# A decoder step on one core: order of loads, operand splits and evictions around the MLP's block products, and the sample's matmuls in runs

## The chip, the core and the metric

The kernel runs on one core of a Trainium2 chip. Its engines take their instructions in program order, each from its own queue: PE (matmuls; its weight loads are PEld), DVE (vector), ACT (scalar), POOL (GpSimd) and SP, which here issues the DMAs. The metric is the device time of one execution in microseconds (us); lower is better.

## The reference

One step of a hybrid decoder trunk with one layer, for a prompt of 1024 tokens and 8 sample tokens which share the weights (`D_MODEL` 1024, `D_FF` 4096, all fp32). Cut to its frame:

```python
h = modulate(x, sh1, sc1)                       # adaLN on an RMS norm
q, k, v, z, xbc, dt_raw = split(h @ w_in)       # one combined projection
attn = merge of three dilated-window attentions over q, k, v
y, h_last = SSD over xbc, dt, starting from state_ssm   # 16 heads x 64 x 128 per sequence
mix = concatenate([rms_norm(attn) * g_attn, rms_norm(y * silu(z)) * g_ssm]) @ w_out
x = x + g1 * mix
u = jnp.square(jax.nn.relu(modulate(x, sh2, sc2) @ w_up))
x = x + g2 * (u @ w_down)
return rms_norm(x) * g_final, caches and states
```

## The kernel before

**Products.** An fp32 product is made of three matmuls of rounded parts (`mm3`): high by high (L63), high by low (L64), low by high (L65). A weight operand is therefore split on the way in: `split` lets ACT cast the high part (L52, tile `oh` for weights, `bo` or `th` for activations) and DVE subtract it from the source to leave the low part (L53, `ol`, `bo`, `tl`). L63 and L64 need the cast, L65 the subtraction too.

**MLP.** Its two matrix products run by a Strassen-Winograd scheme, with seven block products for each pair `q` of weight tiles (16 pairs). A product of the up projection is 4 k-steps of `mm3`, 12 matmuls into one PSUM bank of 128x512; six such banks rotate. The operands of the seven products are the blocks a11, a12, a21, a22 of two weight tiles `mr` and differences of them that POOL forms in place (L1825 to L1831). The generator `up_prep` does for each `q`: load the next pair, the sample tokens' matmuls on the raw tiles (`sample_up`, 16 matmuls with 32 rows), the differences, and one split at each `yield`. `step()` asks it for the next split; `need(key)` asks until that operand is there. For `q` below `EARLY` = 4 the first two products of each pair are done ahead (they need no transformed activations), so the rounds 0 to 3 have five products and the other twelve have seven.

**Order in a round.** `product` (L1978) issues the 12 matmuls, calling `hook(k)` behind each k-step, and then the eviction of the bank, `evict` (L1929): DVE adds the PSUM bank to a partial sum, and for four of the seven products `square` lets ACT do a ReLU and a square in place (L1923, L1924). In the loop over `q` and `j` the hook calls `step()` at k = 1, and at k = 0 and 2 `pop_later`, which issues what the evictions put off into the list `later`: POOL's differences of activations and SP's stores of them to DRAM (`u_d`). The products done ahead for `q` = 2 and 3 run beside `t_prep`, which forms the transformed activations ("hops" 2 to 6) and splits them, one tile at a hook.

**Seam.** In the last up round, `first_b(j)` starts the down projection: `b_pump` and `r_pump` issue loads of activation blocks (tiles `ub`) and of down weights (tiles `mr`) as slots allow, `b_split` splits an activation block. `down_prep` is the generator of the down projection's operands: for each chunk `c` of up to four pairs, product `j` and pair `k` it pumps both lists, calls `sample_down` for the sample's matmuls of a raw weight tile (4 matmuls, into one bank `sd`), splits the weight operand, forms POOL's differences, and splits the activation block.

**Down projection.** `phase_down` runs, for each chunk and product, four row blocks `m` of up to 48 matmuls; behind each it calls `step()`, evicts (adds into `U`, `V3`, `V5`, `P0`, or `gate`: the gated residual into `x1`, L2150), and pops up to five of `later`. In the last chunk the eviction of product 5 puts four POOL adds and four gates for each `m` into `later`. Then the last pair `q` = 15 is done without the scheme ("n" products, three PSUM banks `macc`), with the final norm between them.

**Two places ahead of the MLP.** `sample_ssd` works through the eight sample sequences' SSD states, one step at a time: each step loads a state (`stS`, 4 slots) and a broadcast row (`bbS`, 3 slots) two steps ahead on SP's queue, in between the loads of `qw_raw` for the q/k columns of the input projection and the stores of the caches. `h2_stats` forms, during the output projection, the row statistics of the second norm: after `wait` units of other work PE sums the squares (L1576), DVE and ACT take the root, and after another wait PE spreads it (L1581).

## Time and profile before

| | us |
|---|---|
| median of three runs | 2003.25 (2003.15 to 2004.2) |
| the profiled execution | 2005.3 |
| its span, first to last instruction | 2003.4 |
| PE busy | 1836.5 (92%) |
| DVE busy | 1221.8 (61%) |
| ACT busy | 802.2 (40%) |
| POOL busy | 711.3 (36%) |

The busy shares are means over the whole span; the stages have different limits. On the time axis of the profile the SSD states are worked on around 640 to 740 us, the output projection ends at about 1211, the first block products run until about 1280, the up projection until 1613, and the down projection until 1928, with the tail behind it. In the rows below an instruction is named by engine, line, operation, output tile <- input tiles, and shape; a bracket gives the engine's idle time just ahead of it and what ended that. A window's row gives the stretch and its length, then for PE, PEld, DVE, ACT and POOL the busy time with the number of instructions, then TensorE's granted clock as a share of its full speed, the mean busy share of the DMA engines, and what they moved. A grouped line gives the number of instructions, their busy time with the mean of one in ns, and the idle time ahead of them by releaser.

### The profile page before, as it was taken

How to read it: one execution, taken by the hardware profiler on the slowest of the kernel's cores; microseconds unless marked ns; L12 is line 12 of the kernel's file. 1: busy time of each engine (PE TensorE's matmuls, PEld its weight loads, DVE VectorE, ACT ScalarE, POOL GpSimd, SP SyncE). 2: the span in 40 equal slices, each digit the busy share in tenths (PEclk: the TensorE clock that was granted, in tenths of full speed). 3: DMA queues.
4: the chain of work that ended last, by engine and by line, in shares of the span. 5: the costliest groups of instructions: out<-in, count | busy, mean ns of one | idle time of the engine just before them, and what ended most of it. 6: DMA issues, size and time to landing. Idle time of an engine off the chain costs nothing.

```text
span 2003.4 us, 32735 instructions
## 1 busy us (share of the span) xinstructions
PE 1836.5 (92%) x12252; PEld 1526.1 (76%) x12252; DVE 1221.8 (61%) x2533; ACT 802.2 (40%) x1875; POOL 711.3 (36%) x590
## 2 busy tenths in 40 slices
PE   5999999999999798998889995899999989999976
PEld 3679999999999796766758984566667758778756
DVE  4613675675776667888634446544444465777896
ACT  3511334354422226877522334334443435334322
POOL 0010143342320644999200123454455440531440
PEclk7999999999999899999999997899999989999988
DMA  9674656466334777884573212688787799898712
GB/s 276 255 269 144 212 160 190 165 190 203 115 116 137 186 204 210 196 212 122 170 234 100 86 58 64 216 269 267 256 270 263 250 373 368 298 337 311 278 57 85
DMA packets 249771, 409.28 MB, mean 204 GB/s; under 512 B 35968, under 2 KB 183040, under 8 KB 243169
## 3 DMA queue, kind: packets, MB, share of 16 engines
q1 hardware_dynamic: 246028, 393.82, 60.4%
q0 software_dynamic: 3376, 13.30, 2.1%
q8 instruction: 96, 1.57, 0.3%
q14 instruction: 63, 0.52, 0.1%
q10 hardware_dynamic: 208, 0.07, 0.0%
HBM read 339.76 MB, written 201.65 MB: 270 GB/s over the span
## 4 chain that ended last, share of the span: by engine, by line
PE 67%; DVE 11%; DMA 7%; ACT 6%; POOL 4%; issue 4%; SPq 1%; POOLq 0%; DVEq 0%; ACTq 0%
PE acc L65 18%; PE acc L63 18%; PE acc L64 17%; DVE ol L53 3%; PE s L1294 2%; PE o L1332 2%; PE pt L1316 2%; DMA aw<-in_w_ada 1%; ACT oh L52 1%; DMA q_d<-ab 1%; ACT ub L1923 1%; PE y_ps L868 1%; PE y_ps L861 1%; DMA dkv<-in_cache_v_win 1%; DMA vw_raw<-in_w_in 1%
## 5 line engine op out<-in xcount | busy, mean ns | idle before, releaser
L53 DVE TENSOR_TENSOR ol<-mr,oh 128x512 fp32r<-128x512 f32 x186 | 164.0, 882 | 128.3 <-ACT oh L52 127.3
L64 PE MATMUL acc<-bo,oh 128*128 128x512 f32 (+1 forms) x484 | 186.6, 385 | 15.1 <-DVE bo L53 15.1
L63 PE MATMUL acc<-bo,oh 128*128 128x512 f32 (+1 forms) x484 | 189.6, 392 | 8.8 <-DVE x L2150 6.6
L63 PE MATMUL acc<-h_hi,cw_hi 128*128 128x352 f32 (+1 forms) x576 | 191.8, 333 | 1.1 <-ACT cw_hi L470 1.1
L65 PE MATMUL acc<-bo,ol 128*128 128x512 f32 (+1 forms) x484 | 185.6, 384 | 0.0
L64 PE MATMUL acc<-h_lo,cw_hi 128*128 128x352 f32 (+1 forms) x576 | 184.1, 320 | 0.0
L65 PE MATMUL acc<-h_hi,cw_lo 128*128 128x352 f32 (+1 forms) x576 | 183.7, 319 | 0.2 <-DVE cw_lo L471 0.2
L63 PE MATMUL acc<-h_hi,qw_hi 128*128 128x256 f32 (+1 forms) x512 | 151.7, 296 | 0.0
L65 PE MATMUL acc<-h_hi,qw_lo 128*128 128x256 f32 (+1 forms) x512 | 146.9, 287 | 2.0 <-DVE qw_lo L471 2.0
L64 PE MATMUL acc<-h_lo,qw_hi 128*128 128x256 f32 (+1 forms) x512 | 147.0, 287 | 0.0
L65 PE MATMUL acc<-th,ol 128*128 128x512 f32 x320 | 129.4, 404 | 14.8 <-DVE ol L53 14.7
L52 ACT CAST bo<-ub 128x512 fp32r<-128x512 f32 x109 | 67.5, 619 | 170.0 <-PE acc L65 150.4
L63 PE MATMUL acc<-th,oh 128*128 128x512 f32 x320 | 130.9, 409 | 4.1 <-ACT oh L52 4.1
L64 PE MATMUL acc<-tl,oh 128*128 128x512 f32 x320 | 125.6, 392 | 0.0
L63 PEld LDWEIGHTS acc<-bo,oh 128*128 128x128 f32 x484 | 93.7, 194 | 38.5 <-issue 14.0
L842 POOL TENSOR_TENSOR dec<-dec,CB 128x512 f32<-128x512 f32 x32 | 49.4, 1544 | 205.5 <-ACT dec L841 193.5
L1309 ACT ACTIVATE P<-P,st 128x256 f32<-128x256 f32 (+1 forms) x256 | 118.5, 468 | 2.9 <-DVE st L1298 2.8
L64 PEld LDWEIGHTS acc<-bo,oh 128*128 128x128 f32 x484 | 93.7, 194 | 33.9 <-DVE bo L53 18.0
L52 ACT CAST oh<-mr 128x512 fp32r<-128x512 f32 x186 | 112.9, 613 | 12.0 <-POOL mr L1826 5.9
L1923 ACT ACTIVATE ub<-ub 128x512 f32<-128x512 f32 x60 | 38.0, 633 | 192.0 <-DVE ub L1946 89.5
L53 DVE TENSOR_TENSOR bo<-ub,bo 128x512 fp32r<-128x512 f32 x109 | 105.7, 970 | 12.1 <-ACT bo L52 12.1
L63 PEld LDWEIGHTS acc<-h_hi,cw_hi 128*128 128x128 f32 x576 | 108.4, 188 | 2.1 <-ACT cw_hi L470 1.4
(493 smaller groups left out, 5038.8 us busy)
## 6 DMA issues: line engine op xcount, KB each, us to landing
out_k_win_sample<-in_cache_k_win SPq DMA_DIRECT2D x120, 512.0 KB
out_v_win_sample<-in_cache_v_win SPq DMA_DIRECT2D x120, 512.0 KB
ub<-u_d SPq DMA_DIRECT2D x109, 256.0 KB
u_d<-ub SPq DMA_DIRECT2D x105, 256.0 KB
mr<-in_w_up SPq DMA_DIRECT2D x34, 512.0 KB
aw<-in_w_ada SPq DMA_DIRECT2D x16, 1024.0 KB
mr<-in_w_down SPq DMA_DIRECT2D x32, 512.0 KB
cw_raw<-in_w_in SPq DMA_DIRECT2D x24, 512.0 KB
```

Of the source, the lines that this page charges most:

```text
L52: self.nc.scalar.copy(hi, src)
L53: (eng or self.nc.vector).tensor_tensor(lo, src, f32(hi), op=OP.subtract)
L63: mm(ps, lhi, rhi, start=first, stop=False)
L64: mm(ps, lhi, rlo, start=False, stop=False)
L65: mm(ps, llo, rhi, start=False, stop=last)
L842: nc.gpsimd.tensor_tensor(dec, dec, CB.unsqueeze(1).to_broadcast([128, 4, 128]), op=OP.mult)
L861: nc.tensor.matmul(y[64 * a:64 * a + 64, 128 * j:128 * j + 128], xdt[:, h], G[:, h], start=True, stop=(c == 0))
L1294: nc.tensor.matmul(s[:, a, u, :ws[u]], cols(q, i + u, i + u + 1)[h], cols(k, lo, hi)[h], start=True, stop=True)
L1309: nc.scalar.activation(P, P, AF.Exp, bias=st[:, i + u, a, 0:1], scale=-1.0, accum_out=st[:, i + u, a, 1:2])
L1316: nc.tensor.transpose(p[:, b, a], Ps[m][:, u, a, 128 * b:128 * b + 128], self.ident)
L1332: nc.tensor.matmul(o[64 * a:64 * a + 64, i % 4], v[:, lo + b, 64 * a:64 * a + 64], PT[:, b, a], start=(b == 0), stop=(b == hi - lo - 1))
L1923: nc.scalar.activation(t, t, AF.Relu)
```

## The change

The state and row loads of `sample_ssd` are issued three steps ahead instead of two, with one more slot each. The waits of `h2_stats` are longer. The first weight loads of `up_prep` are issued when the generator is made. In `phase_up`, a product's eviction is held and issued behind the first k-step of the next product; the split of the next operand moves from behind the second k-step to behind the first, ahead of that eviction, and `later` is popped at k = 1 and 3; for `q` = 3 of the products done ahead the split moves from behind the product into it. In the last up round the loads of the down projection start one product earlier, eight activation blocks are split where there were four, and `need((0, 0, 2))` stands ahead of the last eviction. `sample_down` is called once for several tiles: in chunk 0 for all eight, in the other chunks once for each half. At the end of the down projection POOL's adds are issued with the eviction, the gates are put off and popped one at a time, also during the "n" products, which have four PSUM banks. The diff, with context left out:

```diff
@@ -1014,15 +1014,15 @@
...
         def load(b):
-            st = sb.tile([128, 8, 128], F32, name="stS", tag="stS", bufs=4)
+            st = sb.tile([128, 8, 128], F32, name="stS", tag="stS", bufs=5)
             nc.sync.dma_start(st, I["state_ssm"][0, b].rearrange("(hp a) p n -> (a p) hp n", a=2))
-            bb = sb.tile([128, 8, 128], F32, name="bbS", tag="bbS", bufs=3)
+            bb = sb.tile([128, 8, 128], F32, name="bbS", tag="bbS", bufs=4)
             nc.sync.dma_start(bb, bass.AP(tensor=self.bc_d.tensor, offset=self.bc_d.offset + b * 128,
...

-        load(0)
-        load(1)
+        for b in range(3):
+            load(b)
         yield 3000
@@ -1036,8 +1036,8 @@
...
                 nc.gpsimd.tensor_tensor(t2, BB, g4(xd[:, :, b]), op=OP.mult)
-                if b + 2 < NB:
-                    load(b + 2)
+                if b + 3 < NB:
+                    load(b + 3)
                 yield 3200
@@ -1568,7 +1568,7 @@
...

-        def h2_stats(n, p, q, wait=5000):
+        def h2_stats(n, p, q, wait=8000):

@@ -1576,7 +1576,7 @@
...
             self.rstd(self.sm, rs[:, :nb], p[:, 0:nb], [128, 4], "r2")
-            yield 2500
+            yield 4000
             for i in range(nb):
@@ -1722,7 +1722,7 @@
...
         eo.close()
-        return lambda p: chain(h2_stats(2, p, p[:, 128:], 4000), h2_cols(2, p[:, 128:], 600))
+        return lambda p: chain(h2_stats(2, p, p[:, 128:], 4500), h2_cols(2, p[:, 128:], 600))

@@ -1769,7 +1769,7 @@
...
         prep = chain(self.up_prep(), self.down_prep())
-        done = set()
+        done = {next(prep)}

@@ -1809,6 +1809,7 @@
...
         load(0)
+        yield None
         for q in range(2, self.EARLY):
@@ -1975,9 +1976,16 @@
...

+        held = []
+
         def product(q, j, ps, w, hook):
-            self.mul(ps, w, hops[j], True, True, hook)
-            evict(q, j, ps)
+            def at(k):
+                hook(k)
+                if k == 0 and held:
+                    evict(*held.pop())
+
+            self.mul(ps, w, hops[j], True, True, at)
+            held.append((q, j, ps))

@@ -1996,9 +2004,13 @@
...
                 need((q, j))
-                product(q, j, bank(), self.ops.pop((q, j)), lambda k: next(side, None))
-                if q == self.EARLY - 1:
-                    step()
+
+                def hook(k):
+                    if k == 0 and q == self.EARLY - 1:
+                        step()
+                    next(side, None)
+
+                product(q, j, bank(), self.ops.pop((q, j)), hook)
         for q in range(16):
@@ -2006,12 +2018,11 @@
...
                 def hook(k):
-                    if k == 1:
+                    if k == 0:
                         step()
-                        next(side, None)
-                    if k in (0, 2):
+                    if k in (1, 3):
                         self.pop_later(1 + len(self.later) // 8)
-                    if q == 0:
+                    if q == 0 or k == 2:
                         next(side, None)
@@ -2019,6 +2030,8 @@
...
                     self.first_b(j)
+        need((0, 0, 2))
+        evict(*held.pop())
         self.pop_later(99)
@@ -2057,11 +2070,13 @@
...
             self.r_cap, self.b_live = 2, len(self.UB.parts) - 4
-        elif j == 2:
             self.b_pump()
...
         elif j > 2:
-            self.b_split((0, 0, j - 3))
+            for k in range(2):
+                self.b_split((0, (j - 3) // 2, 2 * (1 - j % 2) + k))
+                if j < 5:
+                    self.b_pump()
         if j == 5:
@@ -2074,16 +2089,15 @@
...
                 for k, q in enumerate(qs):
+                    if c or j > 1:
+                        self.b_pump()
                     if c + j:
-                        self.b_pump()
                         self.r_pump()
                     r1 = self.r_raw[c, 0, k]
-                    if j == 0:
-                        self.sample_down(2 * q, r1)
-                    else:
+                    if j:
                         r2 = self.r_raw[c, 1, k]
-                    if j == 1:
-                        self.sample_down(2 * q + 1, r2)
+                    if k == 0 and j < 2 and c + j:
+                        self.sample_down([(2 * p + h, self.r_raw[c, h, i]) for h in ((0, 1) if c == 0 else (j,)) for i, p in enumerate(qs)])
                     if j == 5:
@@ -2098,31 +2112,25 @@
...
                         self.r_live -= 1
-                    if c + j:
+                    if c or j > 1:
                         self.b_split((c, j, k))
...
             r = self.r_raw["n", i // 2]
-            if i % 2 == 0:
-                self.sample_down(30 + i // 2, r)
+            if i == 0:
+                self.sample_down([(30 + h, self.r_raw["n", h]) for h in range(2)])
             self.ops["n", i] = self.split_op(r[:, (lo, hi)[i % 2]])
...

-    def sample_down(self, slot, r):
-
-        if self.sdown is None:
-            self.held_s.append((slot, r))
-            return
-        for s, w in (*self.held_s, (slot, r)):
+    def sample_down(self, tiles):
+
+        for s, w in tiles:
             for j in range(4):
...
                                       start=(s == 0), stop=(s == 31))
-        self.held_s = []
-
-    held_s, sdown = [], None

@@ -2160,11 +2168,15 @@
...
             if j == 5 and c == len(self.CHUNKS) - 1:
-                add = lambda o, a, b: lambda: nc.gpsimd.tensor_tensor(o[:, m], a[:, m], b[:, m], op=OP.add)
-                self.later += [lambda: gate(m, h0, P0[:, m]), add(U, U, P0),
-                               lambda: nc.sync.dma_start(P0[:, m], self.x1_d[:, m + 4, h1]),
-                               add(V3, V3, U), add(U, U, V5), lambda: gate(m, h1, V3[:, m]), add(V3, V3, V5),
-                               lambda: gate(m + 4, h0, U[:, m]), lambda: gate(m + 4, h1, V3[:, m])]
+                for o, a, b in ((U, U, P0), (V5, U, V5), (U, U, V3), (V3, V3, V5)):
+                    nc.gpsimd.tensor_tensor(o[:, m], a[:, m], b[:, m], op=OP.add)
+                if m == 3:
+                    def c11(m):
+                        gate(m, h0, P0[:, m])
+                        nc.sync.dma_start(P0[:, m], self.x1_d[:, m + 4, h1])
+
+                    self.later += [lambda m=m: c11(m) for m in range(4)]
+                    self.later += [lambda m=m, t=t: gate(m + t[0], t[1], t[2][:, m]) for t in ((0, h1, U), (4, h1, V3), (4, h0, V5)) for m in range(4)]

@@ -2183,22 +2195,22 @@
...
                             evict(c, j, m, pss[m])
-                            self.pop_later(5)
+                            self.pop_later()
                             self.background()
...
                     del self.ops[c, j, k], self.b_ops[c, j, k]
-        self.pop_later(99)
         need(("n", 3))
         st = self.pool(el, "fin", bufs=2)
+        nc.scalar.copy(self.sa[:, 0:256], self.sdown[:, 0:256])
         ep.close()
+        esm.close()
         fps = self.pool(ep, "fps", bufs=4, space=PSUM)
-        acc = self.pool(ep, "macc", bufs=3, space=PSUM)
+        acc = self.pool(ep, "macc", bufs=4, space=PSUM)
         gb = st.tile([128, D], F32, name="gb", bufs=1)
...
         def sample_out():
-            nc.scalar.copy(ss[:, 0:256], self.sdown[:, 0:256])
             yield 1500
@@ -2220,6 +2232,7 @@
...
                 gate(m, slice(a, e), ps)
+                self.pop_later()
                 fin.advance(800)
@@ -2230,7 +2243,6 @@
...
         ep.close()
-        esm.close()

```

## Rows read from the trace of the kernel before

**Rows 1.** windows of three stages: us, busy by engine, PEclk, DMA, GB/s

```profile
1613.00:1654.00 41.00, 33.38 (x160) 21.84 (x160) 26.18 (x26) 15.44 (x29) 22.81 (x15) 0.83 1.01 374
1654.00:1928.00 274.00, 274.00 (x1313) 213.46 (x1313) 206.33 (x274) 108.38 (x203) 87.58 (x52) 1.00 0.81 296
1928.00:1960.00 32.00, 19.50 (x84) 15.28 (x83) 28.93 (x37) 1.22 (x3) 13.80 (x9) 0.73 0.10 33
```

**Rows 2.** windows of one early round and of ten later rounds, up projection

```profile
1281.13:1300.21 19.08, 16.34 (x92) 11.53 (x92) 9.78 (x12) 6.47 (x11) 11.36 (x9) 1.00 0.95 320
1357.24:1587.34 230.10, 218.12 (x1168) 161.17 (x1168) 106.92 (x145) 93.87 (x166) 110.61 (x81) 1.00 0.79 263
```

**Rows 3.** timeline of PE in a product: start, us, instruction, [idle <-releaser]

```profile
1422.25 0.39 PE L63 MATMUL acc<-th,oh 128*128 128x512 f32 x1
...
1424.29 0.39 PE L63 MATMUL acc<-th,oh 128*128 128x512 f32 x1
...
1425.37 0.39 PE L64 MATMUL acc<-tl,oh 128*128 128x512 f32 x1
1426.44 0.50 PE L65 MATMUL acc<-th,ol 128*128 128x512 f32 x1 [0.69 <-DVE ol L53]
```

**Rows 4.** timeline of PE around the sample's runs, down projection

```profile
1624.08 1.07 PE L2121 MATMUL sd<-mr,uS 128*32 128x256 f32 x16
1625.08 0.50 PE L63 MATMUL acc<-bo,oh 128*128 128x512 f32 x1
...
1703.82 0.39 PE L65 MATMUL acc<-bo,ol 128*128 128x512 f32 x1
1704.14 0.64 PE L2121 MATMUL sd<-mr,uS 128*32 128x256 f32 x8
...
1705.04 0.39 PE L64 MATMUL acc<-bo,oh 128*128 128x512 f32 x1
```

**Rows 5.** timeline of ACT around 1424, in the up projection

```profile
1423.84 0.63 ACT L1924 ACTIVATE ub<-ub 128x512 f32<-128x512 f32 x1
1424.38 0.60 ACT L52 CAST oh<-mr 128x512 fp32r<-128x512 f32 x1
```

**Rows 6.** lines of DVE, 1339 to 1613: busy us, mean ns, idle before them

```profile
L53 DVE TENSOR_TENSOR ol<-mr,oh 128x512 fp32r<-128x512 f32 x71 | 66.4, 935 | 80.7 <-ACT oh L52 79.9
...
L53 DVE TENSOR_TENSOR ol<-ms,oh 128x512 fp32r<-128x512 f32 x12 | 8.2, 682 | 0.0
```

**Rows 7.** timeline of PE at the first block products

```profile
1253.64 0.79 PE L63 MATMUL acc<-h_hi,oh 128*128 128x512 f32 x1 [21.61 <-ACT oh L52]
...
1262.34 0.50 PE L63 MATMUL acc<-th,oh 128*128 128x512 f32 x1 [2.10 <-ACT oh L52]
```

**Rows 8.** timelines of DVE and of ACT at the first block products

```profile
1241.93 6.66 DVE L53 TENSOR_TENSOR tl<-x,th 128x512 fp32r<-128x512 f32 x4
...
1252.97 0.62 ACT L52 CAST oh<-mr 128x512 fp32r<-128x512 f32 x1
```

**Rows 9.** timeline of PE around the row statistics

```profile
1197.62 0.81 PE L1576 MATMUL otr<-ones,sq 128*128 128x1 f32 x4 [3.11 <-POOL sq L1670]
...
1205.39 0.66 PE L1581 MATMUL otr<-ident,r 128*128 128x128 f32 x2 [2.94 <-DVE r L78]
```

**Rows 10.** timelines of SP and of POOL at the end of the up projection

```profile
1598.15 1.68 SPq L2039 DMA_DIRECT2D mr<-in_w_down  x2
...
1605.52 1.52 POOL L2094 TENSOR_TENSOR ms<-mr 128x512 f32<-128x512 f32 x1 [6.12 <-DMA mr<-in_w_down]
```

**Rows 11.** timeline of PE in the tail

```profile
1934.88 0.79 PE L64 MATMUL acc<-bo,oh 128*128 128x512 f32 x1 [5.45 <-DVE bo L53]
```

**Rows 12.** lines of DVE in the tail, 1914 to 1955

```profile
L2150 DVE SCALAR_TENSOR_TENSOR x<-U,mod,x 128x512 f32<-128x512 f32 x12 | 12.6, 1079 | 1.7 <-POOL U L2163 1.7
L53 DVE TENSOR_TENSOR ol<-mr,oh 128x512 fp32r<-128x512 f32 x8 | 8.7, 1088 | 0.0
```

**Rows 13.** waits of SP's queue, 640 to 740: us in total, times, longest us

```profile
SPq L1018 <- DMA out_ssm_sample<-stS: 14.6, 4, 6.0
```

## What the change is predicted to do, and how

> **What bounds the kernel now.** I read first the windows by stage, because the change touches only some of the 2003 us. Each line of that view gives a stretch's length, PE's busy time in it and the granted clock [rows 1]. From 1654 to 1928 us (the block products of the down projection) PE is busy all the time: only fewer PE slots help there. Over the seam between up and down projection (1613 to 1654) PE is busy 33.38 of 41.00 us at a clock of 0.83, and in the tail (1928 to 1960) 19.50 of 32.00, with DVE busy 28.93: DVE sets the time there. The second window view takes ten whole rounds of the up projection and one early round [rows 2]; PE looks nearly full in both, so "busy" doesn't show the loss and starts have to be counted. For that I read the timelines, PE's first (where does the start-to-start step grow, and who released it), then the timeline of the engine that is named there. Last come the grouped lines of DVE and the waits of SP.
>
> A time here is one of the profiled execution: 2005.3 us, its span 2003.4. The median of the runs is 2003.25, so gains are taken from 2003.25 as they stand. About 0.2% (4 us) is what a measurement of this kernel can tell from no change.
>
> **The change part by part.**
>
> *Up rounds (evict held until after the first quarter of the next product; the next split issued before it).* In a product PE starts a matmul every 0.227 us: nine starts from 1422.25 to 1424.29 take 2.04 [rows 3]. Ten rounds hold 70 products of 12, 840 matmuls, 190.4 us. The rest of their 1168 matmuls is the sample's [rows 2]: a run of 16 costs PE about 1.21 (1.00 from its start to the next product's, and 0.1 at either border [rows 4]), ten in all 12.1; some transposes are estimated at 1.1. Together 203.6, so of 230.10 there are 26.5 lost, 2.65 in each round. The loss sits in one pattern: ACT works in order, the cast `oh` of the next operand at 1424.38 stands behind the two activations of `square` that the evict issued [rows 5], DVE's subtraction `ol` waits for it, and PE's L65 waits for `ol` (0.69 at 1426.44, where the step from the matmul before it, at 1425.37, is 1.07 [rows 3]). In the whole stage DVE stood 79.9 us ahead of `ol` for that cast [rows 6], most of it hidden. After the change cast and subtraction are issued ahead of the evict, about 2.7 us before the product that needs them; the evict in its turn waits on ACT and DVE behind them, and behind the evict only the next one, with five more accumulators free. The pop of POOL's differences a quarter later delays stores, which have `later` to hide them. Only operand (q,2), which needs two POOL differences, stays marginal; I keep 0.2 of the 2.65. For 11.5 rounds (12 less the first's start and the last's end): 2.45 × 11.5 = 28. The three early rounds 1 to 3 have 60 matmuls and one sample run, 14.8, but one takes 19.08 [rows 2]. They are also held by the chain of POOL's differences (11.36 busy of 19.08), which stays; I take 17.6, a gain of 1.5 each, 4.5 in sum. **Up rounds: 32.5, from 24 (a third of the loss stays) to 37 (none).**
>
> *First block products (split issued inside the product).* PE idles 21.61 until 1253.64 and 2.10 until 1262.34, both on a cast `oh` [rows 7]. That cast (1252.97) is queued behind the operand casts of `t_prep` for hops 2, 3 and 4 and DVE's four subtractions (6.66 us from 1241.93) [rows 8]. Issued inside the product, it stands behind two of these hops: DVE is through at 1248.6, and with a subtraction of 0.68 [rows 6] PE starts about 1249.6, 4 earlier; the 2.10 goes, as its POOL difference is issued before and not behind the sample run. **6.5, from 3 to 10.**
>
> *h2_stats (longer waits).* PE waits 3.11 at 1197.62 for POOL's squares and 2.94 at 1205.39 for DVE [rows 9]. The longer wait puts the first behind 3 us more of products, so it goes; the second stays or is paid later. **3, from 0 to 6.**
>
> *First weight loads hoisted.* They are next in SP's queue as it is. **0.**
>
> *Sample's matmuls in runs.* A run of 8 between two products takes 1.22 from L65 at 1703.82 to the second matmul behind it at 1705.04; two matmul slots of 0.227 off that, 0.77. A run of 16 costs 1.21, so a merge of two saves 0.33 [rows 4]. Chunks 1 and 2 lose 6 borders each, chunk 3 loses 4: 16 × 0.33 = 5.3, where PE is busy throughout (274.00 of 274.00 [rows 1]). **5.3, from 4 to 6.**
>
> *Seam (first_b, down_prep).* The block splits of (0,1,k), 8 instructions, move into the last up round, and the pumps with them: each is a 256 KB load on SP's queue, ahead of stores of `u_d`. Of the 160 matmuls of the seam 96 are products and 64 are four runs of the sample's: 96 × 0.227 + 4 × 1.2 = 26.6 of bare work, so about 14 of its 41 us are lost [rows 1]. Against that: `need((0,0,2))` now stands ahead of the last evict, so that evict's ACT and DVE instructions queue behind the split of an operand whose weight tile may not have landed: a pair issued at 1598.15 released POOL at 1605.52, after 6.12 of idling, 7.4 us for the landing [rows 10]. Behind the evict wait the last stores and the pools' release; and the run of 8 tiles now waits for the last tile of the second half. **2, from −8 (that landing once in the open) to +5** (a third of the 14); I choose near the middle, since both mechanisms stand in the same 41 us.
>
> *Tail (adds at once on POOL, gates one at a time, a fourth bank).* DVE has 28.93 of 32.00 busy [rows 1] and does the same gates and splits after as before. What can go is its 1.7 of waiting for POOL's sums and about 0.8 of PE's 5.45 at 1934.88 [rows 11, 12]. The 16 adds in a row on POOL may slow DVE's splits, which take 1.088 in the mean there and 0.682 where POOL is quiet [rows 6, 12]. **2.5, from −2 (a dozen instructions slower by some 0.2) to +6 (the 5.45).** The Trainium skill ("SBUF — State Buffer", Who interferes with whom) says that a VectorE instruction with two inputs in SBUF and a GpSimd instruction that reads SBUF lock each other out for the whole instruction. The 0.682 against 1.088 agree; it speaks against this part and against the splits set beside POOL's differences, and is the mechanism of rival 1: without it the sum is the 51.8 below, by it rival 1's 36.
>
> *State loads three ahead.* In that stage SP waits 14.6 us in four waits, at most 6.0, until a state slot's store has drained [rows 13]; a fifth slot shortens these. The steps' number and POOL's work stay as they are. **0, from −6 (the longest of these waits moved onto the weight loads behind it) to +6 (the same wait gone from the path).**
>
> Sum: 32.5 + 6.5 + 3 + 5.3 + 2 + 2.5 + 0 = 51.8, so 2003.25 − 51.8 = 1951. With every low end 15 remain (1988), with every high end 76 (1927).
>
> **The rivals.**
>
> *1. Splits meet POOL (0.18).* `ol` now comes at the time of POOL's differences and is slower beside them (0.935 mean in this stage, 0.682 alone [rows 6]). If that eats half of the steady rounds' gain, 1.3 × 11.5 = 15 instead of 28, and the early rounds' 4.5 falls to 2: 2003.25 − 36 = 1967. For it: POOL is busy 110.61 of 230.10 [rows 2]. Against it: 2.7 us of slack for one slow subtraction.
>
> *2. The seam and the state loads cost (0.10).* The landing of 7.4 shows, and 6 is lost to the loads: 51.8 − 10 − 6 = 36, also about 1967.
>
> *3. More is freed (0.05).* The early rounds fall to 15 (+8), the seam and the first products give their high ends (+3, +4), h2 too (+3), and the tail gives 6 (+3.5): 51.8 + 21.5, about 1930.
>
> *4. Only the order of issue moves (0.03).* If the engines' waits, not their order, set the rounds (POOL's chain in each), all is hidden: 2003, within 0.2%. Against it: the cast's releaser is its own queue.
>
> *5. Slower (0.04).* A third pair of state loads stands in SP's in-order queue; where its slot is not free, the weight loads of the input projection behind it wait. There are eight steps; the gain of 52 is used up if each step is held by 6.5 us more than now, and 8 us more in each would give 2003.25 − 52 + 64 = 2015. Today's waits of 14.6 in all, 6.0 the longest [rows 13], with one slot more, speak against it.
>
> **How the numbers follow.** The terms hold (1938 to 1968): 0.60; rivals 1 and 2, 0.28, both at 1967 with a spread to 1980; rival 3, 0.05; rivals 4 and 5, 0.07. The forecast is 1951. Leaving out rivals 4 and 5, the slow half of the spread of 1 and 2, and part of 3, the range is 1930 to 1980. Faster by over 0.2%: 0.60 + 0.28 + 0.05 = 0.93; within it 0.03; slower 0.04.
>
> **What would show it.** In the profile of the changed kernel: ten steady rounds in about 206 us instead of 230.10, with ACT's `oh` ahead of the activations and no wait of L65 for `ol`; an early round near 17.6; the first block product's wait near 17.5 instead of 21.61; no wait for POOL's squares; 16 fewer runs of the sample's matmuls between 1654 and 1928, each remaining one of 16 taking 1.0 or longer; the seam not longer, with POOL's wait on the weight tile ahead of the last evict; the tail's DVE as busy as before, with no wait for POOL. Wrong it would be if the rounds stay above 215 (rival 1, if `ol` is then longer; rival 4, if not), if the seam grows past 41 (rival 2), or if the stretch from 640 us on gets longer (rival 5).

## The result, and the profile after

The changed kernel takes 1949.36 us in the median of four runs (1946.67 to 1951.71) against 2003.72 for the kernel before (2003.15 to 2004.54): a ratio of 0.9728, 95% interval 0.9711 to 0.9745. Its profiled execution took 1947.37 us, its span 1945.2. So the two traces differ by 58.2 us and the medians by 54.4; the rest is the choice of the executions.

PE issues its product matmuls in the same order in both kernels, so each of them can be found in both timelines. The table takes the start of the first matmul of each stretch and compares the lengths.

| stretch, with PE's start before / after | before | after | difference | term of the sum |
|---|---|---|---|---|
| to the SSD states' stage (625.15 / 623.45) | 625.15 | 623.45 | −1.7 | none |
| states, attention, first part of the output projection (to 1176.51 / 1177.30) | 551.36 | 553.85 | +2.5 | 0 |
| row statistics, to the first product of `q` = 2 (1223.10 / 1222.15) | 46.59 | 44.85 | −1.7 | −3 |
| first block products, to round 1 (1281.13 / 1274.76) | 58.03 | 52.61 | −5.4 | −6.5 |
| early rounds 1 to 3 (to 1337.53 / 1330.75) | 56.40 | 55.99 | −0.4 | −4.5 |
| rounds 4 to 15, to the last up product (1609.81 / 1572.51) | 272.28 | 241.76 | −30.5 | −28 |
| seam, to the end of the third down product (1665.17 / 1622.51) | 55.36 | 50.00 | −5.4 | −2 |
| down products, to the last of chunk 3 (1928.37 / 1880.26) | 263.20 | 257.75 | −5.5 | −5.3 |
| tail, to the end of the span (2003.4 / 1945.2) | 75.03 | 64.94 | −10.1 | −2.5 |

The sum is −58.2. The first line holds nothing that the change touches. The windows of the changed kernel for one early round, ten later rounds, the seam, and the tail ahead of and behind the first product of the last pair (columns as in the rows ahead of the prediction):

```profile
1274.76:1293.07 18.31, 16.38 (x92) 11.54 (x93) 8.92 (x12) 6.47 (x11) 11.06 (x9) 1.00 0.75 238
1351.12:1556.07 204.95, 204.95 (x1173) 166.11 (x1172) 116.60 (x144) 95.86 (x167) 118.13 (x80) 1.00 0.88 295
1572.51:1622.51 50.00, 41.45 (x221) 32.04 (x220) 30.74 (x35) 22.58 (x41) 23.76 (x15) 0.93 0.98 363
1880.26:1895.75 15.49, 8.34 (x38) 6.57 (x36) 15.49 (x17) 0.74 (x2) 10.61 (x7) 0.88 0.21 70
1895.75:1945.20 49.45, 36.32 (x266) 33.54 (x266) 39.30 (x96) 12.98 (x41) 0.00 (x0) 0.88 0.24 86
```

Before, the same two stretches of the tail were:

```profile
1928.37:1950.61 22.24, 12.00 (x45) 8.06 (x44) 21.72 (x24) 0.85 (x2) 13.43 (x9) 0.77 0.15 48
1950.61:2003.40 52.79, 35.61 (x266) 33.37 (x266) 35.74 (x89) 12.89 (x41) 0.00 (x0) 0.87 0.22 81
```

Ten rounds take 204.95 us against 230.10 [rows 2], and PE is busy in all of it. The early round, 18.31 against 19.08, has gained next to nothing. In the tail DVE is busy without a gap until the last pair's first product (15.49 of 15.49; before 21.72 of 22.24), and that stretch is 6.75 us shorter. Behind it DVE has more to do (39.30 against 35.74) in less time (49.45 against 52.79).

ACT's timeline in a steady round after the change, and DVE's group of weight subtractions from 1330 to 1573 us (lines view, as in [rows 6]):

```profile
1386.06 0.63 ACT L1924 ACTIVATE ub<-ub 128x512 f32<-128x512 f32 x1 [3.05 <-DVE ub L1947]
1386.72 0.63 ACT L1925 ACTIVATE ub<-ub 128x512 f32<-128x512 f32 x1
1387.26 0.60 ACT L52 CAST oh<-mr 128x512 fp32r<-128x512 f32 x1
```

```profile
L53 DVE TENSOR_TENSOR ol<-mr,oh 128x512 fp32r<-128x512 f32 x71 | 78.5, 1109 | 78.8 <-ACT oh L52 77.5
```

The cast still runs directly behind a pair of activations [rows 5], but behind the pair of one product earlier: it is through at 1387.86, when PE has the last matmuls of its product and a run of the sample's (at 1388.65) still ahead of it. The subtraction has become slower, 1.109 us in the mean against 0.935, and DVE's idle time ahead of it, 77.5 against 79.9, has hardly changed [rows 6]. Neither matters any more: PE waits for none of it.

### The profile page after: what moved, and what is told of

Same layout as the page of the kernel before. It is cut to its first block, busy times and chain, and to the rows that moved or that the text cites. A ratio compares the mean times of both kernels' runs of the same rounds, so it can differ in the third digit from the quotient of the medians.

```text
span 1945.2 us, 32764 instructions
## 1 busy us (share of the span) xinstructions
PE 1808.9 (93%) x12252; PEld 1535.4 (79%) x12252; DVE 1230.5 (63%) x2533; ACT 804.7 (41%) x1875; POOL 719.7 (37%) x590
## 4 chain that ended last, share of the span: by engine, by line
PE 67%; DVE 11%; DMA 7%; POOL 6%; ACT 4%; issue 3%; SPq 2%; DVEq 0%; ACTq 0%; POOLq 0%
PE acc L63 19%; PE acc L65 18%; PE acc L64 18%; POOL dkv L1111 2%; POOL dkv L1115 1%; PE s L1294 1%; PE pt L1316 1%; PE o L1332 1%; DVE tl L53 1%; DMA q_d<-ab 1%; DVE ol L53 1%; PE y_ps L868 1%; DVE x L2158 1%; PE y_ps L861 1%; DMA vw_raw<-in_w_in 1%
## 5 line engine op out<-in xcount | busy, mean ns | idle before, releaser
L53 DVE TENSOR_TENSOR ol<-mr,oh 128x512 fp32r<-128x512 f32 x186 | 180.6, 972 | 133.8 <-ACT oh L52 127.8
L63 PE MATMUL acc<-bo,oh 128*128 128x512 f32 (+1 forms) x484 | 185.6, 383 | 14.4 <-DVE x L2158 8.1
L64 PE MATMUL acc<-bo,oh 128*128 128x512 f32 (+1 forms) x484 | 183.5, 379 | 3.0 <-DVE bo L53 3.0
L64 PEld LDWEIGHTS acc<-h_lo,cw_hi 128*128 128x128 f32 x576 | 108.4, 188 | 0.6
L65 PEld LDWEIGHTS acc<-h_hi,cw_lo 128*128 128x128 f32 x576 | 108.2, 188 | 0.5 <-DVE cw_lo L471 0.5
```

Source lines behind the costliest of these rows:

```text
L53: (eng or self.nc.vector).tensor_tensor(lo, src, f32(hi), op=OP.subtract)
L63: mm(ps, lhi, rhi, start=first, stop=False)
L64: mm(ps, lhi, rlo, start=False, stop=False)
L65: mm(ps, llo, rhi, start=False, stop=last)
```

## The experiments

Each is an edit of the changed kernel, unless the text says otherwise. Medians within 3 us of each other are not told apart here, since the runs of one kernel spread by up to 8 us; what a single edit does is read from the stretches of the traces.

### The changed kernel once more

> The changed kernel once more, as the base for the variants beside it and to see where its own runs, which spread from 1946.67 to 1951.71 us, differ. If the spread comes from one place (theory: the order in which DMAs land in the SSD states' stage, 640 to 745 us, or at the start), this execution's PE starts differ from those of the first trace by up to 5 us there and by under 0.3 us in every up round, the seam and the tail. If the block products themselves vary, the rounds differ too.

Measured: 1949.2 us (1944.35 to 1951.49), ratio 0.9717 (0.9703 to 0.9732). The steady rounds, down products and the tail agree with the first trace to 0.05 us each. What differs is the states' stage with what follows (554.72 against 553.85 us), round 3 (18.14 against 19.33) and the seam (51.70 against 50.00). So the theory held for the steady rounds and the tail, and not for round 3 and the seam. Differences in the former are worth reading to a tenth, those in the seam only above 2 us.

### The split behind the held eviction again

```diff
                 def hook(k):
-                    if k == 0:
+                    if k == 1:
                         step()
```

> The changed kernel, but in the rounds 0 to 15 of the up projection the split of the next operand is issued behind the second k-step, so behind the held eviction and its two activations again; the eviction stays held. Theory 1 (the order of cast and activations on ACT's queue makes the steady rounds' gain): the rounds return from about 20.4 to about 22.9 us, some 28 us slower in 11 rounds, about 1977. Rival (holding the eviction, or popping POOL's differences a quarter later, makes the gain): the rounds stay near 20.4 and the time near 1949.

Measured: 1987.17 us, ratio 0.9909 (0.9896 to 0.9923). Ten rounds:

```profile
1360.95:1590.10 229.15, 218.19 (x1170) 161.18 (x1168) 111.55 (x144) 93.85 (x166) 110.59 (x81) 1.00 0.78 264
```

That is 229.15 us, where the kernel before had 230.10 [rows 2] and the changed kernel has 204.95. Holding the eviction and popping POOL's differences later gives 1 us of the 25; the place of the split, ahead of the activations on ACT's queue or behind them, gives the rest. The forecast was 28 us for the whole. The medians differ by 38, the traces of this kernel and the changed one beside it by 35.4: 29.2 in the rounds 4 to 15, 1.7 in the rounds 1 to 3, 4.2 in round 0 and the product ahead of it. Round 0 was not in the expectation.

### The split two products ahead, evictions not held

```diff
                     if k == 0:
-                        step()
+                        step(2 if (q, j) == (0, 2) else 1)
...
                 product(q, j, bank(), self.ops.pop((q, j)), hook)
+                if (q, j) != (15, 6):
+                    evict(*held.pop())
```

> The changed kernel, but evictions are not held in the rounds 0 to 15 (issued right behind their product, as in the kernel before) and the split is asked for two products ahead instead of one. Theory 1 in its general form (what counts is that cast and subtraction are through before the product that needs them): steady rounds at 20.4 or less, as the split still stands behind an eviction but has a whole product (2.7 us) more; the early rounds 1 to 3, 18.3 us each now, may fall towards 16, since POOL's chain starts a product earlier; the time 1941 to 1950. Rival (the eviction must stand behind the split, since the activations wait on PE's last matmul and hold the queue): steady rounds near 22.9, about 1977.

Measured: 1943.71 us, ratio 0.9694 (0.968 to 0.9707). An early round and ten later rounds:

```profile
1273.97:1288.94 14.97, 14.97 (x94) 12.01 (x92) 8.64 (x11) 6.74 (x12) 11.93 (x9) 1.00 0.90 299
1341.18:1546.51 205.33, 205.33 (x1173) 166.24 (x1172) 105.10 (x145) 95.30 (x168) 110.79 (x80) 1.00 0.89 291
```

The steady rounds take 205.33, as with the held eviction, so the rival falls: what counts is only that the split is through before its product, whichever way it is brought forward. The early round shown falls to 14.97, which is the bare work of 14.8; over the rounds 1 to 3 it is 46.8 us against 56.0 and 54.7 in the two traces of the changed kernel. What holds these rounds after the change shows in DVE's, ACT's and POOL's timelines of the changed kernel:

```profile
1274.74 1.23 DVE L53 TENSOR_TENSOR ol<-mr,oh 128x512 fp32r<-128x512 f32 x1 [6.04 <-ACT oh L52]
1275.89 0.68 DVE L1958 TENSOR_TENSOR ub<-acc,t 128x512 f32<-128x512 f32 x1
```

```profile
1274.09 0.62 ACT L52 CAST oh<-mr 128x512 fp32r<-128x512 f32 x1 [4.06 <-POOL mr L1827]
1276.60 0.63 ACT L1924 ACTIVATE ub<-ub 128x512 f32<-128x512 f32 x1 [1.89 <-DVE ub L1958]
1277.26 0.63 ACT L1925 ACTIVATE ub<-ub 128x512 f32<-128x512 f32 x1
1277.80 0.60 ACT L52 CAST oh<-mr 128x512 fp32r<-128x512 f32 x1
```

```profile
1270.16 1.29 POOL L1952 TENSOR_TENSOR ub<-ub,b 128x512 f32<-128x512 f32 x1 [12.37 <-ACT ub L1925]
...
1272.76 1.29 POOL L1827 TENSOR_TENSOR mr<-mr,ms 128x512 f32<-128x512 f32 x1
```

The split of operand (q,2) waits for a POOL difference (L1827). That one stands in POOL's queue behind an operation on activations out of `later` (L1952), which has waited 12.37 us for ACT's activations (5.31 and 5.32 in rounds 1 and 2). Only in round 3, where the split is round 4's, is it the sample's matmuls that POOL waits for (5.67). The split now stands ahead of an eviction whose bank is long done, so DVE idles 6.04 us with that eviction (L1958) behind it, and the next cast, at 1277.80, comes behind the late activations. This idling ahead of a ready eviction is new with the order. Asked for two products ahead, POOL's differences are issued ahead of L1952 (the first at 1267.56, that one at 1273.67) and no longer wait for the activations.

The gain of 10 us up to the last up product was partly lost at the seam (54.72 us against 50.00 and 51.70).

### One part of the change alone, on the kernel before

The eviction held, the split at the first k-step, the pops a k-step later; nothing else.

> The kernel before with one part of the change alone: in the up projection the eviction held, the split issued ahead of it behind the first k-step, the pops a k-step later. Nothing else. Theory 1: the steady rounds fall from 22.9 to 20.4 and the first block products as little as they may (the split stays behind the product there), so 28 us less in the rounds 4 to 15 and the time 1974 to 1978; seam and tail as in the kernel before, or the seam up to 3 longer as the last eviction comes later. Rival (other parts of the change share in the rounds' gain): rounds over 21.

Measured: 1977.36 us, ratio 0.986 (0.9847 to 0.9874).

```profile
1358.06:1563.04 204.98, 204.98 (x1173) 166.09 (x1172) 116.79 (x144) 95.73 (x167) 117.63 (x80) 1.00 0.88 295
```

Ten rounds take 204.98; from round 4 to the last up product it is 30.5 us less than before, exactly as in the whole change (−30.5). Seam, down products and the tail ahead of the last pair are as before within 1 us. The part stands alone and adds up with the rest.

### No request ahead of the last eviction

```diff
-        need((0, 0, 2))
         evict(*held.pop())
```

> The changed kernel without the request for operand (0,0,2) ahead of the last eviction of the up projection. Theory (the last eviction stands on DVE behind two splits whose weight tiles land late; PE's first down product waits 6.15 us for that eviction, the 8 us low end of the seam term): that wait falls to 1 to 2 us, and 3 to 5 us of it remain as a gain at the third block product, so 1944 to 1947 against 1949. Rival (the seam is bound by the loads behind it, so the request costs nothing net): the first wait falls but later waits of the same stage take it back, within 1 us at the third block product; or the next splits come later and it is slower by up to 3.

Measured: 1948.55 us, ratio 0.9722 (0.9707 to 0.9736), not to be told from the changed kernel. PE's and DVE's timelines of the changed kernel at that place, and PE's without the request:

```profile
1581.64 0.76 PE L63 MATMUL acc<-bo,oh 128*128 128x512 f32 x1 [6.15 <-DVE ub L1971]
```

```profile
1579.61 1.28 DVE L53 TENSOR_TENSOR ol<-mr,oh 128x512 fp32r<-128x512 f32 x2
1580.81 0.68 DVE L1971 TENSOR_TENSOR ub<-acc,u 128x512 f32<-128x512 f32 x1
```

```profile
1581.72 0.76 PE L63 MATMUL acc<-bo,oh 128*128 128x512 f32 x1 [4.93 <-DVE ub L1971]
```

The wait falls from 6.15 (7.88 in the second trace) to 4.93 and not to 1 or 2, because the eviction stands behind block splits of `first_b` too (on DVE they are from 1579.68 to 1580.97 in this run, the eviction starts at 1580.89). The seam takes 48.82 us against 50.00 and 51.70: 1 to 3 us, at the edge of what the seam's own spread allows.

### The old order of the activation blocks

The loads and splits in `first_b` and `down_prep` as before: four blocks split in the last up round, not eight.

> The changed kernel with the loads and splits of activation blocks in the last up round as before (four blocks split there, those of the second product's operands in the down projection). Theory (these four splits on ACT and DVE, issued while PE had no slack, are what the second block product of the down projection waited for, 20.55 us against 10.87 in the traces with the change): that product returns to 17 to 21 us, 6 to 10 slower, and the first gets up to 2 shorter. Rival (merging the sample's matmuls, or the earlier landing of loads, is what shortened it): it stays under 13.

Measured: 1955.0 us, ratio 0.9763 (0.9744 to 0.9782). The second down product in the kernel before, in the changed one and here:

```profile
1633.74:1654.29 20.55, 15.12 (x53) 11.07 (x50) 18.34 (x17) 8.19 (x16) 12.03 (x8) 0.75 1.03 393
```

```profile
1597.90:1608.78 10.88, 10.88 (x50) 9.01 (x48) 10.05 (x9) 6.09 (x11) 10.80 (x8) 1.00 1.09 401
```

```profile
1600.01:1618.52 18.51, 13.69 (x50) 10.36 (x48) 18.51 (x15) 6.62 (x13) 17.10 (x11) 0.82 1.04 396
```

It goes from 10.88 back to 18.51, with DVE busy in all of it, and the seam to 57.6 us. DVE was the bound of that product. Four subtractions less stand there now; beside POOL, which is busy 17.10 of the 18.51 us here, one takes about 1.75, so four make 7.0 of the 7.6 us. PE's granted clock is also higher with them gone (1.00 against 0.82 and 0.75).

### The tail's gates as before

The adds and gates put off together, popped five at a time and all ahead of the last pair; four banks and the early copy stay.

> The changed kernel with the tail's gates and adds put off and popped as in the kernel before (five at a time, all of them ahead of the last pair's products); four banks and the early copy of the sample's sum stay. Theory (twelve of the gates now run behind the start of the last pair's products, where DVE has room; ahead of it DVE sets the time, so what counts is the place of the gates and not their number): the stretch from the last chunk's product 6 to the first product of the last pair, 15.5 us now and 22.2 before, returns to 21 to 22, and the rest of the tail stays near 40.7 (44.1 before) or gains up to 2, so 5 to 7 slower than the changed kernel. Rival (the fourth bank carries the tail's gain): that stretch stays under 17 and the time within 2 us.

Measured: 1956.7 us, ratio 0.9766 (0.975 to 0.9782). The two stretches of the tail:

```profile
1882.66:1906.32 23.66, 12.08 (x38) 8.58 (x36) 23.13 (x27) 0.74 (x2) 12.98 (x8) 0.74 0.14 45
1906.32:1954.30 47.98, 35.51 (x266) 33.04 (x266) 33.64 (x86) 12.99 (x41) 0.00 (x0) 0.89 0.24 89
```

The first is 8.2 us longer than in the changed kernel, the second 1.5 shorter. So the place of the gates, with that of POOL's adds, which this edit moves too, makes 7 of the tail's 10 us. The rest (52.79 to 47.98 behind the last pair's first product, less what the first stretch is longer than the 22.24 of before) comes from the fourth bank, the early copy or both; these were not taken apart. In the groups of DVE ahead of the last pair, first before (from 1928.37 us), then after (from 1880.26):

```profile
L2150 DVE SCALAR_TENSOR_TENSOR x<-U,mod,x 128x512 f32<-128x512 f32 x8 | 8.7, 1122 | 0.5 <-POOL U L2163 0.5
...
L2150 DVE SCALAR_TENSOR_TENSOR x<-x,mod 128x512 f32<-128x512 f32 x2 | 3.5, 1758 | 0.0
```

```profile
L2158 DVE SCALAR_TENSOR_TENSOR x<-U,mod,x 128x512 f32<-128x512 f32 x3 | 2.6, 857 | 0.0
L2158 DVE SCALAR_TENSOR_TENSOR x<-x,mod 128x512 f32<-128x512 f32 x2 | 2.2, 1121 | 0.0
```

The ten put-off gates in this stretch, 12.2 us, have become five, 4.8 us. Nine of the sixteen now run behind the last pair's first product (one begins just ahead of it), where POOL does nothing, and take 0.741 in the mean. The expectation's "twelve" is not what the trace has.

### Two ahead, no request, and no gate ahead of the last pair

```diff
                             evict(c, j, m, pss[m])
-                            self.pop_later()
```

and the edits of the runs "The split two products ahead, evictions not held" and "No request ahead of the last eviction".

> Three edits on the changed kernel: evictions not held and the split two products ahead (as in the run of that alone), no request for operand (0,0,2) ahead of the last eviction, and none of the put-off gates issued ahead of the last pair's products (all of them popped between these). Theory: the first gives 9 to 10 us up to the last up product and loses up to 5 of them at the seam, where the last eviction again stands behind late weight tiles; the second gives those back; the third takes four gates of about 1.1 us out of the DVE-bound stretch, 15.5 to some 11 to 12 us. Sum 9 + 2 + 4 = 15 less than 1949, 1934. Rival (the tail's first gates then wait for the reload of the block that they use as scratch; the seam is bound by loads): 1941 to 1944, no better than the first edit alone.

Measured: 1941.12 us, ratio 0.9688 (0.9674 to 0.9703). The tail:

```profile
1872.95:1882.15 9.20, 8.33 (x38) 6.60 (x36) 9.20 (x10) 0.74 (x2) 8.89 (x6) 1.00 0.00 0
1882.15:1938.50 56.35, 36.19 (x266) 32.47 (x266) 45.07 (x102) 12.98 (x41) 1.91 (x2) 0.92 0.28 95
```

The first stretch falls to 9.20, and the second grows by 6.9: sum 65.55 against 64.94 in the changed kernel. The run with the split two ahead alone, which keeps the changed kernel's tail, has 65.57 (15.48 and 50.09), so moving the last gates out gives nothing. The rival was right in its result, by another way: PE now waits for DVE at the final norm's transposes behind the last pair's products. With all gates ahead of the last pair (71.64) DVE is the bound there; with some ahead or none the tail is equally long.

### Two ahead, every eviction first

As two ahead, with the last eviction too right behind its product and no request ahead of it.

> The changed kernel with the split two products ahead and every eviction of the rounds 0 to 15, the last one too, issued right behind its product; no request for operand (0,0,2) ahead of the last one; the tail as in the changed kernel. Theory (in the two runs with the split two ahead the last eviction stood behind block splits that waited for their loads, and PE's first down product waited 8.09 us for it): the first down product starts 2 to 5 us earlier than there, counted from the last up product (11.1 us), the 10 us up to there stay, so 1935 to 1938 against 1949. Rival (the splits of the first two down operands come as late anyway): the start moves by under 1 us, 1940 to 1942.

Measured: 1942.02 us, ratio 0.9686 (0.9673 to 0.9699). The wait of PE's first down product, in the run above and here, and the seam here:

```profile
1573.48 0.77 PE L63 MATMUL acc<-bo,oh 128*128 128x512 f32 x1 [8.09 <-DVE ub L1971]
```

```profile
1571.65 0.76 PE L63 MATMUL acc<-bo,oh 128*128 128x512 f32 x1 [5.27 <-DVE ub L1971]
```

```profile
1563.41:1616.30 52.89, 44.30 (x222) 33.46 (x220) 32.45 (x37) 22.36 (x41) 23.55 (x15) 0.90 1.03 391
```

Counted from the last up product the first down product starts after 8.2 us instead of 11.1, as the theory had it, and the seam still takes 52.89 against 52.79: later products give the 2.8 back, and the time is the rival's. The DMA engines are busy throughout (1.03), as they were before (1.01 [rows 1]). That the loads bound the seam once the up projection ends earlier is argued from this and was not tried by itself.

### Four differences on DVE instead of POOL

```diff
-            g(t2[k], b21[k], t2[k], op=OP.subtract)
+            v(t2[k], b21[k], t2[k], op=OP.subtract)
```

on the kernel of the run above.

> The kernel with the split two products ahead and every eviction first, and besides four differences of t_prep (128x512, L1898) on DVE instead of POOL. Theory (rival 1's mechanism, a subtraction with two inputs in SBUF and a POOL instruction take turns; in the changed kernel's round 0 five subtractions beside these four take 1.75 us instead of 0.68): the subtractions there take 0.68, the four differences cost DVE 2.7 us, and round 0 gets 1.5 to 3 us shorter. Rival (DVE is the bound of round 0 and the four more instructions cost what the others gain; or PE waits there for POOL's other differences): round 0 within 1 us or up to 2.7 longer.

Measured: 1940.68 us (1933.21 to 1941.36), ratio 0.9661 (0.9642 to 0.9679). DVE's timeline in the changed kernel, while POOL runs the four differences from 1251.00 to 1257.79, and then in this one:

```profile
1251.51 1.75 DVE L53 TENSOR_TENSOR ol<-mr,oh 128x512 fp32r<-128x512 f32 x1
1253.18 5.76 DVE L53 TENSOR_TENSOR tl<-x,th 128x512 fp32r<-128x512 f32 x4
```

```profile
1252.98 0.68 DVE L53 TENSOR_TENSOR ol<-mr,oh 128x512 fp32r<-128x512 f32 x1
1253.58 0.68 DVE L53 TENSOR_TENSOR tl<-x,th 128x512 fp32r<-128x512 f32 x1
1254.18 0.68 DVE L1898 TENSOR_TENSOR ub<-x,ub 128x512 f32<-128x512 f32 x1
```

The subtractions take 0.68 instead of 1.75, and a difference that took POOL 1.70 takes DVE 0.68. From the product (3,1) to round 1 it is 1.9 us shorter than without the edit, of which round 0 itself, for which the theory named 1.5 to 3, has 0.4; the seam takes as much back (54.78 against 52.89), so the PE starts behind the seam are 0.3 apart. Against the run without it the medians are not clearly apart (0.9661 and 0.9686, intervals that overlap). Against the changed kernel (0.9728, 0.9711 to 0.9745, and 0.9717, 0.9703 to 0.9732) this version is faster: its interval lies below both. So does that of the run before it (0.9673 to 0.9699), by less; those of the two other runs with the split two ahead overlap or touch the second at its edge.

### State loads two steps ahead

> The changed kernel with the SSD states' loads two steps ahead and one slot fewer each, as before. Theory (a third pair of state loads in SP's queue holds the weight loads of the input projection, rival 5 in small; the stage loses 2 to 5 us against the kernel before in every trace of the changed kernel so far): PE's starts from 625 to 724 us are as in the kernel before, 98.6 us, and the time falls by 2 to 4 us, to 1945 to 1947. Rival (the difference there is the spread of DMA landings from run to run): the stage stays within 1.5 us of 102, the time near 1949.

Measured: 1949.93 us, ratio 0.973 (0.9714 to 0.9747): no difference in the medians. The stretch from 625 to 724 us is 93.3 long, shorter than even before, and gives most of that back behind. From 625 us to the row statistics it is 551.4 us before, 551.5 here and 551.0 in the run of one part alone, all with two steps ahead; the eleven traces with three steps ahead have 553.2 to 557.8. In the waits (us in total, times, longest us) from 640 to 740 us, ACT's wait for the input projection's weights is, in the kernel before, the changed one and this one:

```profile
ACT qw_hi L470 <- DMA qw_raw<-in_w_in: 8.0, 2, 4.4
```

```profile
ACT qw_hi L470 <- DMA qw_raw<-in_w_in: 17.6, 3, 9.3
```

```profile
ACT qw_hi L470 <- DMA qw_raw<-in_w_in: 6.2, 2, 3.2
```

It is 15.4 to 19.0 in all eleven traces with three steps ahead and 6.2 to 8.0 in the three with two. ACT's wait for the states themselves goes the other way, in the kernel before and the changed one:

```profile
ACT stS L1037 <- DMA stS<-in_state_ssm: 23.5, 5, 7.4
```

```profile
ACT stS L1037 <- DMA stS<-in_state_ssm: 15.0, 2, 7.6
```

So the third pair of state loads does what it was put there for, and holds the weight loads; with three steps ahead the stretch up to the row statistics is longer by 1.7 to 6.8 us in every trace. The medians don't show it. They don't tell 3 us apart, and in the trace of this run the first 625 us, which the edit leaves alone, took 626.18 against 623.45 and 624.41 in the changed kernel's two.

### The old waits of h2_stats

> The changed kernel with the waits of h2_stats as before. Theory (the longer waits take POOL's wait of 3 us away and leave or pay DVE's later; 2 us net in every trace of the changed kernel, counted from 1177 us to the first early block product): that stretch is 2 us longer again, 46.6 instead of 44.6 to 44.9, and the time 1 to 3 us more, within the spread of its runs. Rival (the wait only moved): the stretch is the same within 0.5.

Measured: 1950.41 us, ratio 0.9729 (0.9715 to 0.9743). PE's waits in the changed kernel, then here:

```profile
1207.15 0.66 PE L1581 MATMUL otr<-ident,r 128*128 128x128 f32 x2 [5.11 <-DVE r L78]
```

```profile
1202.98 1.01 PE L1576 MATMUL otr<-ones,sq 128*128 128x1 f32 x4 [3.11 <-POOL sq L1670]
...
1210.76 0.66 PE L1581 MATMUL otr<-ident,r 128*128 128x128 f32 x2 [1.94 <-DVE r L78]
```

The stretch takes 47.9 us against 44.6 and 44.9: the longer waits are worth 3 us against this run, and 1.7 against the kernel before, which with the same waits as here took 46.59. The wait for POOL's squares is gone with them, and the second has grown from 1.94 (2.94 before, [rows 9]) to 5.11, so PE's idle time in all is the same, 5.05 here and 5.11 in the changed kernel. The 3 us lie elsewhere, as the windows of the stretch show, the changed kernel's first:

```profile
1177.30:1222.15 44.85, 39.74 (x269) 36.70 (x268) 27.84 (x68) 23.88 (x46) 8.34 (x11) 0.92 0.37 101
```

```profile
1181.93:1229.85 47.92, 42.87 (x268) 40.05 (x267) 28.95 (x70) 24.47 (x48) 8.93 (x11) 0.86 0.35 94
```

PE is busy 3.1 us longer with as many matmuls, at a mean granted clock of 0.86 instead of 0.92. With 1.0 and 0.5 as the two levels that is some 13 us at the lower one (1.2 GHz) against 7, behind two idle times here and behind one there.

## Why the prediction was right, and where its steps failed

The forecast was 1951 with a range of 1930 to 1980, and 1949.36 came. The main case held, and its largest term for the reason given.

- **Steady rounds.** Forecast 28, measured 30.5 in the whole change, 30.5 alone, and lost again when only the split's place was undone. The step was right to the pattern. Ten rounds took 204.95, 1.35 more than the bare work worked out there, where 2.0 were kept for operand (q,2). The rest of the difference is the count of rounds, nearly 12 and not 11.5, and round 4, which alone gained 3.0.
- **Early rounds.** Forecast 4.5, measured 0.4 (1.7 in the second trace). The step that failed is the sentence on what the evict waits on: it was taken to wait harmlessly behind the split. Where the split itself waits for POOL, DVE idles 6.04 us ahead of an eviction that was ready, and the next cast comes late again. POOL's chain, which the prediction had as staying, was held by an operation out of `later` at its head. Asking two products ahead showed that 8 to 9 us could be had there.
- **First block products.** Forecast 6.5, measured 5.4, by another way. The wait of 21.61 [rows 7] fell to 11.08, not 17.5: behind two hops only, and ahead of most of POOL's differences, three of DVE's four subtractions took 0.68. The split inside the product goes with it: in the run of one part alone, which leaves that out, product (3,1) starts 24.0 us behind (3,0), against 14.0 here and 24.9 before. In return round 0 took 26.1 us instead of 18.8, since the later hops now met them. The term was near in the sum (its two parts, 4 and 2.1, make 6.1 and not 6.5) and wrong in its parts.
- **h2_stats.** Forecast 3, measured 1.7 in the trace and 3 against the run with the old waits. The first wait went and the second was paid later, as said, but PE's idle time fell by only 0.9 against the kernel before (6.05 to 5.11), and against the run with the old waits by nothing. The 3 there are time at the lower granted clock, for which the prediction had no term.
- **Sample's runs.** Forecast 5.3, measured 5.5. 23 runs became 7, the 16 fewer that were named, and PE has no idle time in that stage in either kernel. No run takes this part alone.
- **Seam.** Forecast 2 from −8 to +5, measured 5.4 and 3.7 in two traces. The wait ahead of the last eviction came (6.15 and 7.88 against 0.86 before, the low end's size), but by another way than the landing that was named: 4.93 of it stays without the request, behind block splits. And the four splits moved out were mis-sized: 9.7 us at the second down product, which DVE bounded (7.6 by the run with the old order), against the 5 taken from a third of the seam's loss.
- **Tail.** Forecast 2.5, at most 6; measured 10.1. The failed step is "does the same gates and splits after as before": the number of instructions is the same, but DVE sets the time only ahead of the last pair, and gates were moved out of that stretch. It is the place that counts, 7 us by the run with the gates back. DVE's work itself also fell by 2.7 (21.72 + 35.74 to 15.49 + 39.30), as a gate that doesn't meet POOL's adds is shorter. The fourth bank and the early copy, with the other 3, had no term in the sum.
- **State loads.** Forecast 0 from −6 to +6; the traces show a loss of 2 to 7, with the longer wait for the weights that rival 5 named, far below the 6.5 a step from which that rival decides.
- **Rival 1** came in its mechanism and not in its price: `ol` is slower (1.109 against 0.935), and PE doesn't wait for it, as the slack of 2.7 us was enough. Where there was no slack, in round 0, the same mechanism cost about 1 us for each subtraction beside a POOL difference.

That the time came within 2 us of the forecast is luck in part. In the traces the early rounds, the first products, the row statistics and the state loads gave 9 less than forecast, and seam and tail 11 more. Without the second the time would have been near 1960. The term for the first weight loads, 0, was not tried by itself.

## What to carry to other kernels

On an engine that works in order, look at what stands ahead of the instruction that the bottleneck waits for, and bring that instruction forward by a whole product; asking further ahead did it as well here as holding back what is in front, and added no wait in the rounds, though the seam took part of that back. Before a moved instruction is costed at nothing, ask what it waits for itself: an instruction that isn't ready blocks a ready one behind it. And where an engine is full in one stretch and not in the next, moving its work across the border can pay, even if the sum of its work doesn't change: here 8.2 us ahead for 1.5 behind, and nothing more for the last gates, for which the other side gave back all.

## What was not expected of the hardware

The 128x512 subtraction on DVE takes 0.68 us alone and 1.75 beside a POOL difference of the same size, which takes 1.70 then and 1.29 alone (POOL's L1952 in the early rounds): a pair takes nearly what the two would one after the other, an estimated 1.97. Four such differences moved onto DVE cost it 0.68 each and returned about 1.07 for each of the subtractions beside them. The Trainium skill ("SBUF — State Buffer", Who interferes with whom) describes this as an exclusive lock between a VectorE instruction with two inputs in SBUF and a GpSimd one that reads SBUF; the rows agree. The gates of the tail, which also read two operands in SBUF, show it too: 1.122 in the mean and up to 1.76 beside POOL's adds, 0.74 without.
